# Attention scores: full passes of 128 rows, and the 32 or 64 rows left over in row groups of the TensorE array

## The chip, the cores and the metric

The kernel runs on one core of one Trainium2 chip. The metric is the device time of one execution in microseconds, as the median of several runs. The profile used below is of one further execution of the same program on the chip.

## The reference, cut to what matters

Two layers of a diffusion backbone are computed in 32-bit floats, over 1024 latent tokens (16 rows of 64) and 256 context tokens. Layer 0 has 8 heads of dense attention (the GQA heads, 64 features, two key heads) and 8 heads of neighbourhood attention (64 features, 8 rows by 16 columns of keys around each query, plus the context). Layer 1 has 16 heads of latent attention (MLA), whose queries and keys have 64 features without and 32 features with rotary embedding. Each attention is followed by a projection, a normalisation and a gated feed-forward layer with a convolution.

```python
HEAD_DIM = 64; A_HEADS = 8; A_KV_HEADS = 2; B_HEADS = 8
MLA_HEADS = 16; MLA_NOPE_DIM = 64; MLA_ROPE_DIM = 32

def one_block(qblk):                                    # dense attention, layers 0 and 1
    s = jnp.concatenate([jnp.einsum('bgrqd,bgkd->bgrqk', qblk, k),
                         jnp.einsum('bgrqd,bgcd->bgrqc', qblk, kc)], axis=-1)
    p = jax.nn.softmax(s.astype(jnp.float32) * scale, axis=-1).astype(v.dtype)
    return (jnp.einsum('bgrqk,bgkd->bgrqd', p[..., :length], v)
            + jnp.einsum('bgrqc,bgcd->bgrqd', p[..., length:], vc))

# neighbourhood attention, one row of queries, layer 0
s_nb = jnp.einsum('bhqd,bhrqkd->bhqrk', q_row, k_win).astype(jnp.float32) * scale + bias[None]
s_ctx = jnp.einsum('bhqd,bhcd->bhqc', q_row, kc).astype(jnp.float32) * scale

# layer 1
q = jnp.concatenate([q_nope, _rope(q_rope, cos, sin)], axis=-1)        # 64 + 32 features
k, v = up_kv(c_kv, _rope(k_r, cos, sin))                               # the 32 are shared by the heads
```

## The kernel before

TensorE works on float32r numbers here, and each 32-bit value that enters a product is split into a high and a low part, so that a product becomes a sum of products of parts. The scores of a head are made that way. For a GQA or neighbourhood head, the query tile `q` holds the 64 features of the high part over the 64 of the low part (128 rows), and the key tile `k` holds, twice, the high part in its first slot and the low part in its second. Two passes of 128 rows are summed: query tile by high keys, and query tile by low keys. For an MLA head the tiles have 96 rows and a slot for each part, and three passes of 96 rows are summed: high by high, high by low, low by high.

`attention()` works in units, a unit being a pair of query tiles of 128 queries. There are 4 units in a head: 32 units of GQA, 32 of the neighbourhood and 64 of MLA, and in layer 0 a context unit after the first pair of every second head. `seg` makes the scores of one query tile against a run of keys: it cuts the run at PSUM banks of 512 columns, and each piece becomes a function `go` that issues all the passes of that piece, one after the other, into its bank. For GQA and MLA the pieces of a unit have 512, 512, 256 (first tile), 256 and 512, 512 (second tile) columns; for the neighbourhood they have 384 and 256, and 256 and 384. The lists `la` and `lb` of these functions are spread over the places `sa` and `sb` of a schedule (`GQA_SCHED`, `NAT_SCHED`, `MLA_SCHED`, in units of a period). All steps of all units go into one heap by those places: scores on TensorE, maximum on VectorE, exponential on ScalarE, scaling on GpSimd, transposes on TensorE (`transpose`, L304), the split of the transposed exponentials (L311 to L320), the weighted sums on TensorE (`weighted`, L335) and the sum into `y` (`finish`). TensorE, ScalarE and VectorE then run in exactly that order.

The heads' tiles are loaded ahead: `prep` and `prep1` of head n + 1 are called with the second unit of head n, on the queue of SyncE (SP). In `prep1` the loads of MLA head 0 go to GpSimd's queue instead and into a pool of their own (`att1f`); those of the other heads use two buffers in turn (`att1k`). Layer 0's first head takes tiles that were loaded during the projections (`first`). The last unit's projections of layer 1 end in `up_q` and `up_kv`, which run through the helper `mm_acc` (L417); its rotary step for the shared key, `prt_k`, is a small product of 32 rows by 32 columns, and L730 spreads a row of four numbers over 128 partitions, with four-row weights.

The two lines by which a score is made:

```python
for pi, (q, k) in enumerate(u["passes"]):
    ...
    nc.tensor.matmul(
        u["s"][bank][:, c:e], q[:, qc], ks, start=pi == 0, stop=pi == len(u["passes"]) - 1
    )
```

Of the kernel before, what the change touches and what calls it, by code (L numbers as in the profile page):

```python
# [18 lines left out]
P = 128  # L19
D = 1024  # L20
# [13 lines left out]
# first of the 32 columns that 16 columns of queries look at  # L34
# [3 lines left out]
# places of the steps of a pair of query tiles, in units of the period  # L38
# [19 lines left out]
def attention(tc, pa, pp, ident, mone, units, engines=("tensor", "scalar", "vector")):  # L58
    """Softmax attention over pairs of query tiles.

    `units` make dicts: qt (query tiles), passes ((queries, keys) products whose sum is the score),
    v ([keys, tile, v_hi | v_lo]), y. A unit with "window" (w, bias) has the neighbourhood's queries of
    the w-th 16 columns, upper half over lower half, each against twelve rows of 32 columns. A unit
    with "context" has the context's queries of two heads and goes between two pairs.
    TensorE makes the scores of a pair, VectorE their maximum, ScalarE the exponentials and their
    sums; TensorE transposes the exponentials, ScalarE and VectorE (or GpSimd) split them into two
    float32r parts on the way out, and TensorE makes the weighted sums, which the reciprocal of
    the sum scales. Units come with a schedule that places these steps in time, in units of
    its period; the engines in `engines` keep that order.
    """  # L70
# [7 lines left out]
    def region(tag, sched):  # L78
        """PSUM for scores (sa, sb), transposed exponentials (t) and weighted sums (av)"""
# [9 lines left out]
    def plan_context(i, u, sched):  # L89
        """both heads' context queries, between two pairs"""  # L90
# [69 lines left out]
        # between the sums of two pairs  # L160
# [5 lines left out]
    def plan(i, u, sc):  # L166
# [11 lines left out]
        def seg(when, bank, c, k0, w, j, rows=None):  # L178
# [3 lines left out]
            lst = []  # L182
            while w:
                e = min(c + w, (c // 512 + 1) * 512)
                def go(c=c, e=e, k0=k0):
                    if bank not in u["s"]:
                        u["s"][bank] = region(bank, sc)
                    for pi, (q, k) in enumerate(u["passes"]):
                        if rows is None:
                            ks = k[:, k0 : k0 + e - c]  # L190
                        else:
                            w0 = WINDOWS[win]
                            ks = k[:, 0:NX].rearrange("p (r c) -> p r c", c=64)[:, rows : rows + 12, w0 : w0 + 32]
                        nc.tensor.matmul(  # L194
                            u["s"][bank][:, c:e], q[:, qc], ks, start=pi == 0, stop=pi == len(u["passes"]) - 1
                        )

                lst.append(go)
                w -= e - c
                k0 += e - c  # L200
                c = e
            when.extend(lst)

        la, lb = [], []
        if win is None:
            seg(la, "sa", 0, 0, 1024, 0)
            seg(la, "sa", 1024, NX, 256, 0)
            seg(la, "sa", 1280, NX, 256, 1)
            seg(lb, "sb", 0, 0, 1024, 1)
            segs = [[("sa", 0, 1280)], [("sb", 0, 1024), ("sa", 1280, 256)]]  # L210
        else:
            seg(la, "sa", 128, 0, 384, 0, rows=0)
            seg(la, "sa", 512, NX, 256, 0)
            seg(lb, "sb", 256, NX, 256, 1)
            seg(lb, "sb", 512, 0, 384, 1, rows=4)
# [58 lines left out]
        # blocks of 128 keys, shared by the query tiles that look at them, in groups of one bank  # L274
# [1639 lines left out]
```

## Time and profile before

| what | us |
|---|---|
| median of 3 runs | 3627.86 |
| lowest and highest run | 3622.21, 3631.36 |
| span of the profiled execution | 3624.5 |
| GQA scores, from the first to the last, on TensorE | 367.8 to 621 |
| neighbourhood scores | 634.3 to 797 |
| MLA scores | 2227.4 to 2739 |

The profiled execution lies 3.4 us below the median of the runs. The page gives busy times of the engines over the whole span; TensorE (PE) is far ahead. A matmul's listed duration runs from its start until its result has drained, so durations of successive matmuls overlap: what a matmul costs in a stream is the distance from its start to the next one's start, and it is read from the timeline. PEld is TensorE's weight load, which precedes every matmul.

### The profile page before, as it was taken

How to read it: one execution, taken by the hardware profiler on the slowest of the kernel's cores; microseconds unless marked ns; L12 is line 12 of the kernel's file. 1: busy time of each engine (PE TensorE's matmuls, PEld its weight loads, DVE VectorE, ACT ScalarE, POOL GpSimd, SP SyncE). 2: the span in 40 equal slices, each digit the busy share in tenths (PEclk: the TensorE clock that was granted, in tenths of full speed). 3: DMA queues.
4: the chain of work that ended last, by engine and by line, in shares of the span. 5: the costliest groups of instructions: out<-in, count | busy, mean ns of one | idle time of the engine just before them, and what ended most of it. 6: DMA issues, size and time to landing. Idle time of an engine off the chain costs nothing.

```text
span 3624.5 us, 50952 instructions
## 1 busy us (share of the span) xinstructions
PE 3444.8 (95%) x19450; PEld 2949.6 (81%) x19450; DVE 2252.0 (62%) x3434; ACT 1281.6 (35%) x2393; POOL 1668.7 (46%) x1804
## 2 busy tenths in 40 slices
PE   7998899979899999999998999999999999999997
PEld 5987787877788888888886787999997788888885
DVE  6687787873666666655455544777774555445555
ACT  4222777762411111111025334777773301111002
POOL 4532787643422222232223523888886533333333
PEclk9999999999999999999999999999999999999998
DMA  6367411664333322211104267233323211111111
GB/s 211 111 203 217 108 46 48 166 181 139 117 108 96 93 88 82 82 53 41 36 19 125 82 242 231 57 79 76 80 66 114 85 47 47 53 47 47 53 35 47
DMA packets 311952, 349.52 MB, mean 96 GB/s; under 512 B 19157, under 2 KB 233597, under 8 KB 311709
## 3 DMA queue, kind: packets, MB, share of 16 engines
q1 hardware_dynamic: 298508, 319.66, 30.4%
q10 hardware_dynamic: 11424, 18.94, 1.4%
q0 software_dynamic: 1776, 7.67, 0.6%
q8 instruction: 153, 2.51, 0.3%
q14 instruction: 91, 0.74, 0.1%
HBM read 275.04 MB, written 71.11 MB: 96 GB/s over the span
## 4 chain that ended last, share of the span: by engine, by line
PE 74%; POOL 8%; DVE 8%; issue 5%; DMA 4%; ACT 2%; SPq 0%; ACTq 0%; POOLq 0%; DVEq 0%
PE pu L417 29%; PE pd L417 15%; PE psum L194 7%; PE psum L335 5%; PE pso L417 4%; PE psum L304 4%; POOL p L264 3%; PE psq L417 2%; PE ps_f L417 2%; PE ps_tu L417 1%; DVE aa L552 1%; PE pw L417 1%; POOL pl L312 1%; DMA bias<-in_l_rpb_dram 1%; POOL st L261 1%
## 5 line engine op out<-in xcount | busy, mean ns | idle before, releaser
L1400 DVE SCALAR_TENSOR_TENSOR acc<-pd,mods,acc 128x512 f32<-128x512 f32 (+1 forms) x800 | 525.0, 697 | 267.0 <-PE pd L417 252.3
L408 POOL TENSOR_SCALAR fh_u<-fr_u 128x1024 fp32r<-128x1024 f32 x88 | 95.0, 1079 | 857.6 <-PE pu L417 479.9
L417 PE MATMUL pd<-ah,fh_d 128*128 128x512 f32 (+1 forms) x880 | 331.7, 377 | 6.3 <-DVE acc L1400 3.8
L417 PE MATMUL pd<-al,fh_d 128*128 128x512 f32 (+1 forms) x880 | 326.0, 370 | 0.5 <-DVE al L412 0.5
L417 PE MATMUL pd<-ah,fl_d 128*128 128x512 f32 (+1 forms) x880 | 325.9, 370 | 0.0
L194 PE MATMUL psum<-k,q 96*128 96x512 f32 (+1 forms) x1152 | 272.3, 373 | 6.7 <-DMA k<-kr_scr 4.0
L417 PE MATMUL pu<-h_1l,fh_u 128*128 128x512 f32 x704 | 275.1, 391 | 2.1 <-POOL h_1l L412 2.1
L417 PE MATMUL pu<-h_0h,fh_u 128*128 128x512 f32 x704 | 275.3, 391 | 0.0
L417 PE MATMUL pu<-h_0h,fl_u 128*128 128x512 f32 x704 | 275.0, 391 | 0.0
L417 PE MATMUL pu<-h_0l,fh_u 128*128 128x512 f32 x704 | 274.9, 391 | 0.0
L417 PE MATMUL pu<-h_1h,fh_u 128*128 128x512 f32 x704 | 274.3, 390 | 0.0
L417 PE MATMUL pu<-h_1h,fl_u 128*128 128x512 f32 x704 | 274.0, 389 | 0.0
L1381 DVE TENSOR_TENSOR cv<-cv,pu 128x1280 f32<-128x1280 f32 (+1 forms) x44 | 59.6, 1355 | 295.7 <-PE pu L417 289.1
L194 PEld LDWEIGHTS psum<-k,q 96*128 96x128 f32 x1152 | 196.4, 192 | 35.3 <-issue 4.4
L412 POOL TENSOR_TENSOR fl_u<-fr_u,fh_u 128x1024 fp32r<-128x1024 f32 x88 | 212.4, 2413 | 7.3
L552 DVE SCALAR_TENSOR_TENSOR aa<-aw,silu_late,aa 128x512 f32<-128x512 f32 x224 | 190.5, 880 | 37.1 <-DMA aw<-in_l_w_ada_dram 34.9
L417 PEld LDWEIGHTS pd<-ah,fh_d 128*128 128x128 f32 x880 | 166.1, 189 | 58.2 <-DVE acc L1400 5.1
L1377 ACT ACTIVATE cv<-cv 128x1280 f32<-128x1280 f32 (+1 forms) x44 | 51.4, 1169 | 443.0 <-DVE cv L1373 443.0
L264 POOL TENSOR_SCALAR p_m<-p_m,st_m 128x640 f32<-128x640 f32 x256 | 201.8, 801 | 12.6
L1367 ACT ACTIVATE cv<-pu,vec 128x1280 f32<-128x1280 f32 (+1 forms) x44 | 58.2, 1322 | 417.5 <-PE pu L417 417.5
L320 DVE TENSOR_TENSOR pl_m<-psum,ph_m 128x512 fp32r<-128x512 f32 x256 | 175.0, 684 | 37.7 <-ACT ph_m L314 36.7
L304 PE MATMUL psum<-ident,p_m 128*128 128x128 f32 x1280 | 192.9, 273 | 2.5 <-DVE pl_m L320 2.2
(499 smaller groups left out, 9817.1 us busy)
## 6 DMA issues: line engine op xcount, KB each, us to landing
aw<-in_l_w_ada_dram SPq DMA_DIRECT2D x96, 512.0 KB
fr_u<-in_l_w_up_dram SPq DMA_DIRECT2D x88, 512.0 KB
fr_d<-in_l_w_down_dram SPq DMA_DIRECT2D x44, 512.0 KB
fr_o<-in_l_w_out_dram SPq DMA_DIRECT2D x30, 512.0 KB
v<-v_scr SPq DMA_DIRECT2D x17, 640.0 KB
k_b<-k_scr SPq DMA_DIRECT2D x16, 640.0 KB
v_scr<-vev SPq DMA_DIRECT2D x40, 256.0 KB
k<-k_scr SPq DMA_DIRECT2D x15, 640.0 KB
```

Source lines behind the costliest of these rows:

```text
L194: nc.tensor.matmul(u["s"][bank][:, c:e], q[:, qc], ks, start=pi == 0, stop=pi == len(u["passes"]) - 1)
L264: nc.gpsimd.tensor_scalar(pt, pt, st[:, j, 7:8], 0.0, op0=ALU.mult, op1=ALU.add)
L304: nc.tensor.transpose(tp[:, off + bi * P : off + bi * P + P], pts[j][:, c : c + P], ident)
L320: nc.vector.tensor_tensor(pl[:, :w], tps[g][:, :w], ph[:, :w].bitcast(F32), ALU.subtract)
L335: nc.tensor.matmul(u["av"][:, q0 : q0 + bw], u["v"][:, kt, :], m[:, off : off + bw], start=first and part == 0, stop=last and part == 1, s ...
L408: nc.gpsimd.tensor_scalar(dst, src, 1.0, 0.0, op0=ALU.mult, op1=ALU.add)
L412: e.tensor_tensor(dst, src, hi.bitcast(F32), ALU.subtract)
L417: nc.tensor.matmul(ps, s, m, start=i == 0, stop=i == n - 1)
L552: nc.vector.scalar_tensor_tensor(accs[c], w, sck, accs[c], op0=ALU.mult, op1=ALU.add)
L1367: nc.scalar.activation(cv, g[:, :nt], AF.Identity, bias=vec(l, "cb", f), scale=vec(l, "w1", f))
L1381: nc.vector.tensor_tensor(cv, cv, v[:, :nt], ALU.mult)
L1400: nc.vector.scalar_tensor_tensor(acc[m][ci], ps[:, :cn], mod(l, ci // 2, 5, m), acc[m][ci], op0=ALU.mult, op1=ALU.add)
```

## The change

The passes of a score become full passes of 128 rows and a remainder, which is a matmul of 64 rows (GQA, neighbourhood) or 32 rows (MLA) of the array.

- GQA and neighbourhood: one full pass, (high over low) queries by high keys, and a remainder of 64 rows, high queries by low keys. The remainder is either on rows 0 to 63, from `q` and `k`, or on rows 64 to 127, from a new tile `ql` that holds the high queries there; pieces take the two in turn. The product of the two low parts is left out. A tile `ql` is loaded for each head, one more transfer of 64 rows. The context's queries keep their two passes.
- MLA: the 3 x 96 = 288 rows are packed into two full passes of 128 rows and a remainder of 32 rows, which is loaded four times, on rows 0, 32, 64 and 96. The tiles get 128 rows and three slots. A head's queries and keys are then loaded by 18 transfers instead of 4, and even and odd heads have one buffer each, in `att1f` and `att1k`.
- Order on TensorE: `seg` returns the full passes and the remainders apart, and `beside` places the remainders of neighbouring pieces behind their full passes as one step. The pieces of a step go to different banks and, as far as there are, to different row groups. Each unit of GQA and MLA has three such steps (of 3, 1 and 2 matmuls), each unit of the neighbourhood two (of 2 and 2).

```diff
-                def go(c=c, e=e, k0=k0):
+                n = n0 + len(lst)
...
+                def go(c=c, e=e, keys=keys):
                     if bank not in u["s"]:
                         u["s"][bank] = region(bank, sc)
                     for pi, (q, k) in enumerate(u["passes"]):
...
+                        nc.tensor.matmul(u["s"][bank][:, c:e], q[:, qc], keys(k), start=pi == 0, stop=False)
+
+                def last(c=c, e=e, keys=keys, n=n):
+
+                    q, k = u["thin"][n % len(u["thin"])]
+                    nc.tensor.matmul(u["s"][bank][:, c:e], q[:, qc], keys(k), start=False, stop=True)
...
+        def beside(*pieces):
+
+            full, thin = zip(*pieces)
+            full, thin = sum(full, []), sum(thin, [])
+
+            def rest():
+                for f in thin:
+                    f()
+
+            return [*full, rest]
+
         if win is None:
-            seg(la, "sa", 0, 0, 1024, 0)
-            seg(la, "sa", 1024, NX, 256, 0)
-            seg(la, "sa", 1280, NX, 256, 1)
-            seg(lb, "sb", 0, 0, 1024, 1)
+            la = beside(seg("sa", 0, 0, 1024, 0, 0), seg("sa", 1024, NX, 256, 0, 2))
+
+            la += beside(seg("sa", 1280, NX, 256, 1, 2))
+            lb = beside(seg("sb", 0, 0, 1024, 1, 0))
             segs = [[("sa", 0, 1280)], [("sb", 0, 1024), ("sa", 1280, 256)]]
         else:
...
+            la = beside(seg("sa", 128, 0, 384, 0, 0, rows=0), seg("sa", 512, NX, 256, 0, 1))
+            lb = beside(seg("sb", 256, NX, 256, 1, 0), seg("sb", 512, 0, 384, 1, 1, rows=4))
...
-            return q
...
+            return q, load_low(src, h, name)
+
+        def load_low(src, h, name):
+            ql = pa.tile([P, NT], F32R, name=f"ql_{name}", tag="ql", bufs=3)
+            nc.sync.dma_start(ql[64:P].bitcast(F32), src[0, 64 * h : 64 * h + 64, :])
+            return ql
...
-                    "passes": [(st["q"], st["k"][0]), (st["q"], st["k"][1])],
+                    "passes": [(st["q"][0], st["k"][0])],
+                    "thin": [(st["q"][0][0:64], st["k"][1][0:64]), (st["q"][1][64:P], st["k"][1][64:P])],
...
-            pool, load = (pk, nc.sync) if hd else (pf, nc.gpsimd)
+            pool, load = pk if hd % 2 else pf, nc.sync if hd else nc.gpsimd
...
-            q = pool.tile([96, 2, NX], F32R, name=f"q1_{hd}", tag="q", bufs=2 if hd else 1)
-            k = pool.tile([96, 2, NT], F32R, name=f"k1_{hd}", tag="k", bufs=2 if hd else 1)
+            q = pool.tile([P, 3, NX], F32R, name=f"q1_{hd}", tag="q", bufs=1)
+            k = pool.tile([P, 3, NT], F32R, name=f"k1_{hd}", tag="k", bufs=1)
...
-                (q[0:64], q1_scr[g][:, 64 * j : 64 * j + 64]), (q[64:96], qr_scr[g][:, 32 * j : 32 * j + 32]),
-                (k[0:64], k1_scr[g][:, 64 * j : 64 * j + 64]), (k[64:96], kr_scr),
+                *((q[0:64, i], qn[:, 0]) for i in range(2)), *((q[64:96, i], qr[:, 0]) for i in range(2)),
+                (q[96:P, 0], qr[:, 1]), (q[96:P, 1], qn[0:32, 1]),
+                (k[0:64, 0:2], kn), (k[64:96, 0:2], kr), (k[96:P, 0], kr[:, 0]), (k[96:P, 1], kn[0:32, 0]),
+                *((q[r : r + 32, 2], qn[32:64, 1]) for r in range(0, P, 32)),
+                *((k[r : r + 32, 2], kn[32:64, 0]) for r in range(0, P, 32)),
...
-                    "passes": [(qh, kh), (qh, kl), (ql, kh)],
+                    "passes": [(q[:, i, :], k[:, i, :]) for i in range(2)],
+                    "thin": [(q[r : r + 32, 2, :], k[r : r + 32, 2, :]) for r in range(0, P, 32)],
```

TensorE, the scores of one MLA unit's list `la`, in the middle of layer 1. In these rows L194 is a score before, `ident,p_m` is a transpose, and `ph_m,v` begins a weighted sum. Before:

```order
L194 MATMUL psum<-k_12_25257,q_12_25256 128x512 x6
L194 MATMUL psum<-k_12_25257,q_12_25256 128x256 x3
L304 MATMUL psum<-ident,p_m_0_0_25663 128x128
L304 MATMUL psum<-ident,p_m_0_1_25640 128x128
L304 MATMUL psum<-ident,p_m_0_0_25663 128x128
L304 MATMUL psum<-ident,p_m_0_1_25640 128x128
L194 MATMUL psum<-k_12_25257,q_12_25256 128x256 x3
L335 MATMUL psum<-ph_m_0_1_25761,v_12_25255 128x256
```

And the same place of another head now, where L198 is a full pass and L203 a remainder:

```order
L198 MATMUL psum<-k_11_25023,q_11_25022 128x512 x4
L198 MATMUL psum<-k_11_25023,q_11_25022 128x256 x2
L203 MATMUL psum<-k_11_25023,q_11_25022 128x512 x2
L203 MATMUL psum<-k_11_25023,q_11_25022 128x256
L198 MATMUL psum<-k_11_25023,q_11_25022 128x256 x2
L320 MATMUL psum<-ident,p_m_0_0_25443 128x128
L320 MATMUL psum<-ident,p_m_0_1_25420 128x128
L320 MATMUL psum<-ident,p_m_0_0_25443 128x128
L320 MATMUL psum<-ident,p_m_0_1_25420 128x128
L203 MATMUL psum<-k_11_25023,q_11_25022 128x256
L351 MATMUL psum<-ph_m_0_1_25555,v_11_25021 128x256
```

Where each piece had three passes in a row, the remainders of the first three pieces now stand together between full passes, and the fourth piece's remainder stands alone between the transposes and the weighted sum.

GpSimd's queue, the loads of MLA head 0 at the start of layer 1's attention, with the semaphores that each waits for (a name with DMASW is the landing of an earlier transfer of this queue, one of eight in turn). Before:

```order
L1783 DMA q_0_20647<-q_scr_103 64x2x1024 [waits DMAHW7_49,PE_49]
L1783 DMA q_0_20647<-qr_scr_107 32x2x1024 [waits DMAHW4_49]
L1783 DMA k_0_20648<-k_scr_111 64x2x1280 [waits Pool_49]
L1783 DMA k_0_20648<-kr_scr 32x2x1280
L1784 DMA v_0_20646<-v_scr_115 128x10x128 [waits DMAHW7_49,DMAHW6_49,DMAHW4_49]
```

Now, the first ten rows of the same place (four more of the queries' remainder, four of the keys' and the values follow):

```order
L1817 DMA q_0_20679<-q_scr_103 64x1024 [waits DMAHW7_49,PE_49]
L1817 DMA q_0_20679<-q_scr_103 64x1024
L1817 DMA q_0_20679<-qr_scr_107 32x1024 x2
L1817 DMA q_0_20679<-qr_scr_107 32x1024 [waits DMAHW4_49]
L1817 DMA q_0_20679<-q_scr_103 32x1024
L1817 DMA k_0_20680<-k_scr_111 64x2x1280 [waits PE_49,Pool_49]
L1817 DMA k_0_20680<-kr_scr 32x2x1280
L1817 DMA k_0_20680<-kr_scr 32x1280 [waits DMASW0_49]
L1817 DMA k_0_20680<-k_scr_111 32x1280 [waits DMASW1_49]
```

From the ninth transfer on, each waits for the landing of the one eight before it.

## Rows read from the trace of the kernel before

**Rows 1.** The page: busy time by engine, and the chain that ended last.
```profile
PE 3444.8 (95%) x19450; PEld 2949.6 (81%) x19450; DVE 2252.0 (62%) x3434; ACT 1281.6 (35%) x2393; POOL 1668.7 (46%) x1804
...
PE 74%; POOL 8%; DVE 8%; issue 5%; DMA 4%; ACT 2%; SPq 0%; ACTq 0%; POOLq 0%; DVEq 0%
```
**Rows 2.** Busy time by stretch: GQA, neighbourhood, steady MLA; then clock, DMA share, GB/s.
```profile
367.00:627.00 260.00, 236.73 (x1676) 208.92 (x1676) 204.60 (x301) 199.62 (x419) 206.96 (x304) 0.99 0.25 62
632.00:803.00 171.00, 147.47 (x1089) 137.26 (x1090) 131.85 (x283) 127.13 (x307) 105.17 (x161) 0.97 0.64 172
2262.00:2705.00 443.00, 443.00 (x3197) 415.68 (x3196) 342.33 (x497) 350.45 (x717) 388.86 (x552) 1.00 0.32 73
```
**Rows 3.** TensorE's waits between 632 and 803 us: total us, times, longest.
```profile
PE psum L335 <- DVE y L368: 10.6, 14, 3.4
```
**Rows 4.** Timeline of TensorE in MLA: start us, duration us, operation, count; 8.04 us apart.
```profile
2452.81 1.63 PE L194 MATMUL psum<-k,q 96*128 96x512 f32 x6
...
2455.12 1.97 PE L194 MATMUL psum<-k,q 96*128 96x512 f32 x9
2456.92 0.60 PE L304 MATMUL psum<-ident,p_m 128*128 128x128 f32 x4
2457.28 0.60 PE L194 MATMUL psum<-k,q 96*128 96x256 f32 x3
2457.72 0.28 PE L335 MATMUL psum<-ph_m,v 128*128 128x256 f32 x1
2457.84 0.28 PE L335 MATMUL psum<-pl_m,v 128*128 128x256 f32 x1
...
2460.85 1.63 PE L194 MATMUL psum<-k,q 96*128 96x512 f32 x6
```
**Rows 5.** Timeline of TensorE in layer 1's first projection, around a 32-row matmul.
```profile
1953.71 0.39 PE L417 MATMUL pw<-h_0h,fh_wi 128*128 128x512 f32 x1
1953.93 0.39 PE L417 MATMUL pw<-h_0l,fh_wi 128*128 128x512 f32 x1
1954.25 0.41 PE L417 MATMUL prt_k<-reh_k,perm 32*32 32x512 f32 x1
1954.59 0.50 PE L417 MATMUL pw<-h_0h,fl_wi 128*128 128x512 f32 x1
1954.93 0.40 PE L417 MATMUL pw<-h_0h,fh_wi 128*128 128x512 f32 x1
```
**Rows 6.** The weight loads of the same place.
```profile
1954.25 0.10 PEld L417 LDWEIGHTS prt_k<-reh_k,perm 32*32 32x32 f32 x1 [0.35 <-issue]
1954.59 0.19 PEld L417 LDWEIGHTS pw<-h_0h,fl_wi 128*128 128x128 f32 x1 [0.24 <-issue]
1954.70 0.19 PEld L417 LDWEIGHTS pw<-h_0h,fh_wi 128*128 128x128 f32 x1
```
**Rows 7.** Timeline of TensorE around eight matmuls of four rows and two columns.
```profile
53.22 0.40 PE L788 MATMUL ps_f<-hh,wl_in 128*128 128x512 f32 x1
53.55 1.05 PE L730 MATMUL ps_mr<-pick,row 4*128 4x2 f32 x8
54.53 0.39 PE L788 MATMUL ps_f<-hh,wh_in 128*128 128x256 f32 x1
```
**Rows 8.** Line L1783, the loads of MLA heads: issue ns, and waits behind them.
```profile
L1783 SPq DMA_DIRECT2D q<-q_scr x15: 586/586/2985, 2230.6 to 2675.0; - x15
...
L1783 POOL DMA_DIRECT2D k<-kr_scr x1: 554/554/554, 2216.5 to 2216.5; - x1
...
  PE psum L194: 4.0, 1
...
DMA to landing us min/median/max: 6.0/8.1/10.8
```
**Rows 9.** One stretch in which MLA head 3 is loaded: clock, DMA share, GB/s.
```profile
2292.00:2294.00 2.00, 1.00 1.11 227
```

More of the change, by code (lines that the diff above doesn't have):

```diff
@@ L176, in plan, with seg, keys @@
         pts = [None] * nq
-        def seg(when, bank, c, k0, w, j, rows=None):
+        def seg(bank, c, k0, w, j, n0, rows=None):
             qc = slice(u["qt"][j] * P, u["qt"][j] * P + P)
-            lst = []
+            lst, thin = [], []
             while w:
                 e = min(c + w, (c // 512 + 1) * 512)
-                def go(c=c, e=e, k0=k0):
+                n = n0 + len(lst)
+                def keys(k, c=c, e=e, k0=k0):
+                    if rows is None:
+                        return k[:, k0 : k0 + e - c]
+                    w0 = WINDOWS[win]
+                    return k[:, 0:NX].rearrange("p (r c) -> p r c", c=64)[:, rows : rows + 12, w0 : w0 + 32]
+                def go(c=c, e=e, keys=keys):
                     if bank not in u["s"]:
@@ L188, in go @@
                     for pi, (q, k) in enumerate(u["passes"]):
[L189 to L196, printed above, removed]
+                        nc.tensor.matmul(u["s"][bank][:, c:e], q[:, qc], keys(k), start=pi == 0, stop=False)
+                def last(c=c, e=e, keys=keys, n=n):
+                    q, k = u["thin"][n % len(u["thin"])]
+                    nc.tensor.matmul(u["s"][bank][:, c:e], q[:, qc], keys(k), start=False, stop=True)
                 lst.append(go)
+                thin.append(last)
                 w -= e - c
@@ L201, in seg @@
                 c = e
[L202 to L204 removed]
+            return lst, thin
+        def beside(*pieces):
[5 more added lines that the diff above has]
+            return [*full, rest]
         if win is None:
[L206 to L209 removed]
+            la = beside(seg("sa", 0, 0, 1024, 0, 0), seg("sa", 1024, NX, 256, 0, 2))
+            la += beside(seg("sa", 1280, NX, 256, 1, 2))
+            lb = beside(seg("sb", 0, 0, 1024, 1, 0))
             segs = [[("sa", 0, 1280)], [("sb", 0, 1024), ("sa", 1280, 256)]]
         else:
[L212 to L215, printed above, removed]
+            la = beside(seg("sa", 128, 0, 384, 0, 0, rows=0), seg("sa", 512, NX, 256, 0, 1))
+            lb = beside(seg("sb", 256, NX, 256, 1, 0), seg("sb", 512, 0, 384, 1, 1, rows=4))
             segs = [[("sa", 128, 640)], [("sb", 256, 640)]]
@@ L1090, in prep @@
                 g = hd // 4
-                st["q"] = load_q(q_scr[hd // 2], hd % 2, f"a{hd}") if hd else first[2]
+                st["q"] = (
+                    load_q(q_scr[hd // 2], hd % 2, f"a{hd}") if hd else (first[2], load_low(q_scr[0], 0, "a0"))
+                )
                 if hd % 4 == 0:
@@ L1132, in make @@
                     st = state[h]
-                    heads.append({"passes": [(st["q"], st["k"][0]), (st["q"], st["k"][1])], "v": st["v"], "vc": 8 if h < 8 else 16})
+                    heads.append({"passes": [(st["q"][0], st["k"][0]), (st["q"][0], st["k"][1])], "v": st["v"], "vc": 8 if h < 8 else 16})
                 return {"name": f"c{hd}", "context": heads, "y": state["y", hd // 2]}
```

8 lines of the change are left out of this document (6 added, 2 removed).

## The prediction

> **What bounds the kernel now.** I read the page first. TensorE is busy for 95% of the span and carries 74% of the chain that ended last [rows 1], so time added to or taken from its stream shows in the end, unless TensorE waits where it falls. I therefore looked at the three stretches that the change touches, by windows [rows 2]. In MLA's steady part TensorE is busy for all of 443 us at a granted clock of 1.00, that is 2.4 GHz: every tenth of a microsecond there counts in full. In the GQA stretch it is not busy for 260.00 - 236.73 = 23 us, in the neighbourhood stretch for 171.00 - 147.47 = 24 us, the largest single wait in the latter being 10.6 us for VectorE's `y` [rows 3].
>
> Then the price of one matmul, from distances between starts. In a stream, 512 columns take 0.225 us (0.22 in [rows 5]) and 256 columns 0.12 [rows 4]. This closes: six of the one and three of the other would be 1.71 us, and from 2455.12 to 2456.92 they take 1.80 [rows 4]; three of 256 would be 0.36 and take 0.44. The extra 0.08 to 0.09 is paid by the first matmul behind a group of transposes. Weight loads are hidden in these streams. An MLA unit takes 2460.85 - 2452.81 = 8.04 us.
>
> **What the change removes.** Only the last pass of each piece. Full passes cost by their columns, so 96 or 128 rows make no difference to their price. The removed passes of an MLA unit are 512, 512, 256 columns (0.57 us), 256 (0.12) and 512, 512 (0.45), 1.14 us in all; GQA's are the same; the neighbourhood's are two times 384 and 256. For 384 I have no undisturbed row and take 0.17, between the other two, so 0.29 each.
>
> **What it adds: the switch.** A remainder is a 32- or 64-row matmul between 128-row ones. The trace has this pattern in a few places, and one is shown: `prt_k`, 32 rows and 512 columns, in a stream of full matmuls of 512 columns [rows 5]. The starts are 1953.93, 1954.25, 1954.59 and 1954.93: three matmuls in 1.00 us where three full ones take 0.675. The 0.32 us more stand in three parts: 0.10 before the small one starts, 0.11 behind it, and 0.11 for the next one's weights. The weight loads say why [rows 6]: the small matmul's load does not start with the matmul before it, as in a stream, but 0.32 us after that, together with its own matmul, and the same holds for the full one behind it. PEld's releaser is "issue", so no data was late. A second example, eight four-row matmuls with 128-column weights, starts 0.33 us behind a 512-column one [rows 7], again 0.10 late. The remainders' weights have 128 columns, `prt_k`'s 32. A load of 128 columns takes 0.11 (1954.59 to 1954.70, [rows 6]), one of 32 a quarter, so 0.08 more is exposed. I price a step of remainders at **0.40 us** besides its columns.
>
> **What it gives: matmuls side by side.** No row shows two row groups at work at once, so this is bounded. At best the matmuls of a step run wholly together and the longest counts; at worst they run one after the other and nothing is saved. I take the middle case, by the row nearest to it: each needs its own 128-column weights, and matmuls of only two columns still follow each other by (54.53 - 53.55) / 8 = 0.12 us [rows 7], close to the load's 0.11. So a second row group starts 0.11 later and a third 0.22.
>
> - MLA, three steps in a unit. 512, 512, 256: 0.11 + 0.225 = 0.34 in place of 0.57, saved 0.23. 512, 512: 0.335 in place of 0.45, saved 0.12. The lone 256 saves nothing. Added 3 x 0.40 = 1.20, less 0.08 at the lone one, which stands behind transposes and had paid that before [rows 4]. Net 1.20 - 0.08 - 0.35 = +0.77 us, times 64 units: **+49 us**.
> - GQA, three steps. There are two row groups, so the third piece returns to the first one's and must wait for its end and its weights: 0.225 + 0.11 + 0.12 = 0.455, saved 0.115; the pair saves 0.115. Net 1.20 - 0.23 = +0.97, times 32: **+31 us**.
> - Neighbourhood, two steps: 0.80, saved 0.06 (384 then 256) and 0.01 (256 then 384). Net +0.73, times 32: **+23 us**.
>
> The Trainium skill's page "TensorE: Matmul & The Clock Gate" (Measured speedup vs the span model) gives 3.07 times for four row groups of 32 rows and 512 columns. That would be a start about 0.02 us after the other (an estimate from that figure) instead of 0.11, and the sum below would be about 18 us smaller. No row here shows it.
>
> **What is moved or loaded.** In MLA a head's queries and keys grow from 96 rows and two slots to 128 rows and three: 3.5 MB instead of 1.8, in 18 transfers instead of 4, with 0.66 MB of values as before. At the 227 GB/s that a head's load reaches now [rows 9] 4.2 MB take 18.5 us, and 18 issues of 0.59 us [rows 8] 10.6 us. A head lasts 4 x 8.04 = 32 us now and longer then, and the buffers change hands as before, so this is hidden; its cover is the head's own scores. What is queued behind a waiting transfer on SP is only the next head's tiles.
>
> The start of layer 1's attention has no cover. Head 0's loads are on GpSimd's queue, 0.55 us each, and land after 6.0 to 10.8 us; TensorE already waits 4.0 us for the last of them [rows 8]. With 18, the ninth may only start when the first has landed, and so on in eights; the first remainder needs the copies on its two row groups, which are among the last. Two rounds of landing in place of one are 8 us (the median), and some of it again for the third. From 3 us (only more bytes) to 15 (two further rounds): I take **+10**. Behind these transfers GpSimd's own queue holds only head 0's first scalings, which need the scores anyway. In layer 0 the first head's `ql` is one transfer more ahead of the first remainder: +1.
>
> Other engines get slack, since TensorE is their source. Where TensorE waited for them, part of its added time disappears in the wait: half of the neighbourhood stretch's 24 us, **-12** (between 0 and all 24).
>
> **Sum.** 49 + 31 + 23 + 10 + 1 - 12 = +102 us on the span of 3624.5, which is 3.4 below the median of the runs: 3627.9 + 102 = **3730 us**. With everything side by side the steps give 35 + 24 + 18 = 77, less 24 of waits, plus 3: +56, 3684. With nothing saved: 72 + 38 + 26 = 136, plus 15: +151, 3779.
>
> **Rivals.**
>
> - The row groups run one after the other and each exposes its weights. Then 3, 3 and 2 loads of 0.11 a unit come on top of "nothing saved", 39 us: about 3800. For it: in [rows 6] a load waits until the array is free. Against: that is at a change between shapes, not between row groups. Chance 0.13.
> - Faster. The switch costs nothing, because the small weights are loaded beside running full matmuls, and the row groups run together. Each MLA unit then loses 0.57 us, each GQA unit 0.45, each neighbourhood unit 0.24: 36 + 14 + 8 = 58 us less, plus 11 at the starts: 3580 us. It decides at a price of the step of about 0.15 us. For it: `prt_k` changes columns too (32), the remainders do not. Against: the four-row matmuls have all 128 columns and start as late [rows 7]. Chance 0.08. The skill's page "TensorEngine Tiling (Array Packing)" (Theoretical Speedup) promises up to 2 or 4 times for 64 or 32 rows; its Key Properties add that a change of tiling mode drains the engine. The 0.10 us before and behind `prt_k` agree with the latter.
> - The switch costs half, 0.20 us, as the schedule puts it where weights are late anyway. MLA +0.17, GQA +0.37, neighbourhood +0.33 a unit: 33 us, with starts and waits 32: 3660 us. Chance 0.08.
> - The MLA loads become the bound, if 32-row transfers, eight at a time, reach only half the rate: 39 us a head, 4 more than the 35 that I expect a head to take, 60 us in all: 3790. Against: a DMA share of 0.32 now [rows 2]. Chance 0.03.
>
> **How the numbers follow.** My forecast, a time between 3684 and 3779, has 0.68. The range runs from 3665, which takes in part of the half-price case, to 3795, which takes in the loads and the lower part of the serial case. Changes below 0.3% (11 us) can hardly be told from none here. Slower by more than that: 0.68 + 0.13 + 0.03 + most of the 0.08, together 0.89. Within: 0.03. Faster: 0.08.
>
> **What the profile of the changed kernel would show.** An MLA unit of about 8.8 us, still with TensorE busy throughout; by 8.6 everything ran side by side, by 9.2 nothing did, and below 8.04 the switch is free. Around each step of remainders, weight loads that start only after the full matmul before, about 0.32 us behind its start, and the same for the full one behind. Inside a step, starts 0.11 us apart. A first MLA score some 5 us later than now and a first remainder some 5 us after that. Neighbourhood waits for `y` mostly gone. The prediction is wrong if a remainder's weights are loaded during the full matmul ahead of it.

## The result, and the profile after

| | before | after |
|---|---|---|
| median of four runs, us | 3625.03 | 3709.47 |
| lowest and highest, us | 3615.21, 3631.36 | 3707.10, 3710.53 |
| span of the profiled execution, us | 3624.5 | 3705.2 |

The changed kernel is slower, by a ratio of 1.0237 with a 95% interval of 1.022 to 1.0255, or 84 us by the medians and 81 by the two profiled executions. The forecast was 3730, the range 3665 to 3795.

The first two parts of the page, which answer [rows 1]. TensorE is as far ahead as before and carries the same share of the chain; it does more.

```profile
PE 3517.4 (95%) x19450; PEld 2905.7 (78%) x19450; DVE 2256.9 (61%) x3434; ACT 1283.9 (35%) x2393; POOL 1676.8 (45%) x1818
...
PE 75%; POOL 8%; DVE 7%; issue 4%; DMA 3%; ACT 2%; ACTq 0%; SPq 0%; POOLq 0%; DVEq 0%
```

The three stretches by windows, as in [rows 2]: GQA, neighbourhood, and MLA in its steady part.

```profile
365.00:640.00 275.00, 253.75 (x1658) 198.55 (x1659) 204.81 (x298) 198.22 (x414) 207.09 (x304) 0.98 0.28 73
649.00:841.00 192.00, 163.88 (x1106) 131.56 (x1104) 135.63 (x285) 129.02 (x311) 103.43 (x159) 0.98 0.59 155
2300.00:2790.00 490.00, 490.00 (x3292) 403.05 (x3291) 351.79 (x511) 360.49 (x738) 399.98 (x566) 1.00 0.55 121
```

MLA is TensorE without a gap, at the same clock. The busy share alone does not prove that (run 10 below is as busy in a slower unit), but the starts do: beyond the 0.61 us that a unit gains they leave no room for waits. TensorE's free time in the two stretches of layer 0, 21 and 28 us, is together no smaller than before (23 and 24). From where each stage begins in the two traces, the 81 us lie as follows: GQA +17.7, neighbourhood +25.7, start of layer 1's attention +3.1, its units +43.1, and -8.8 at the start of the program and between the layers. Of the neighbourhood's 25.7, 18.1 lie between its first score and its last weighted sum, and 7.6 between that sum and the first matmul of layer 0's projection. An MLA unit takes 8.647 us instead of 8.04, a GQA unit 7.80 instead of 7.27, a neighbourhood unit 4.78 instead of 4.05 to 4.17.

The steps of remainders, on the timeline of TensorE (start us, duration us, operation, count): an MLA unit with its three steps and the beginning of the next unit, 8.65 us later, and the weight loads (PEld) of the last place, as in [rows 6].

```profile
2495.41 1.17 PE L198 MATMUL psum<-k,q 128*128 128x512 f32 x4
...
2499.21 0.50 PE L203 MATMUL psum<-k,q 32*128 32x512 f32 x3
2499.64 0.51 PE L198 MATMUL psum<-k,q 128*128 128x256 f32 x2
2499.98 0.60 PE L320 MATMUL psum<-ident,p_m 128*128 128x128 f32 x4
2500.51 0.38 PE L203 MATMUL psum<-k,q 32*128 32x256 f32 x1
2500.82 0.39 PE L351 MATMUL psum<-ph_m,v 128*128 128x256 f32 x1
...
2504.06 1.17 PE L198 MATMUL psum<-k,q 128*128 128x512 f32 x4
2505.16 0.50 PE L203 MATMUL psum<-k,q 32*128 32x512 f32 x2
2505.59 0.39 PE L351 MATMUL psum<-ph_m,v 128*128 128x256 f32 x1
2505.81 0.28 PE L351 MATMUL psum<-pl_m,v 128*128 128x256 f32 x1
```

```profile
2504.61 0.19 PEld L198 LDWEIGHTS psum<-k,q 128*128 128x128 f32 x1
2505.16 0.18 PEld L203 LDWEIGHTS psum<-k,q 32*128 32x128 f32 x2 [0.36 <-issue]
2505.59 0.19 PEld L351 LDWEIGHTS psum<-ph_m,v 128*128 128x128 f32 x1 [0.25 <-issue]
```

L203 is a remainder. Two remainders of 512 columns take 0.50 us together, as long as one: they and their weights start within 0.004 us of each other. The last step starts 0.318 us behind the start of the last full matmul (0.225 in a stream), the next matmul 0.43 behind the step, and its successor 0.22 behind that instead of 0.12. That is 0.09 ahead, 0.20 behind and 0.10 for the next weights: **0.39 us for a step**, where the forecast had 0.40. The whole unit gives the same. It is 0.61 us longer, without the 1.14 of its third passes and with 0.225 + 0.225 + 0.12 = 0.57 of remainder columns, so 1.18 us stand for three steps. The expectations below went by 0.42, a figure that counts 0.08 too much at the lone step behind the transposes (see the price of a step, further down).

GQA, whose third piece has to return to the first one's row group:

```profile
583.81 0.49 PE L203 MATMUL psum<-k_a,q_a 64*128 64x512 f32 x1
583.82 0.50 PE L203 MATMUL psum<-k_a,ql_a 64*128 64x512 f32 x1
584.15 0.28 PE L203 MATMUL psum<-k_a,q_a 64*128 64x256 f32 x1
584.36 0.39 PE L198 MATMUL psum<-k_a,q_a 128*128 128x256 f32 x1
```

Neighbourhood: VectorE's rows of a unit, and then TensorE's waits in the stretch (us in all, times, longest us), as in [rows 3].

```profile
701.83 0.82 DVE L250 CUSTOM_DVE_ANT_0 p<-psum,bias 128x640 f32<-128x640 f32 x1 [0.48 <-PE psum L203]
...
704.11 0.82 DVE L250 CUSTOM_DVE_ANT_0 p<-psum,bias 128x640 f32<-128x640 f32 x1 [0.33 <-PE psum L203]
704.86 0.08 DVE L250 DVE_READ_ACCUMULATOR2_ANT st<- 128x1 f32 x1
704.99 0.42 DVE L384 TENSOR_TENSOR y<-psum,avt 64x256 f32<-64x256 f32 x1
```

```profile
PE psum L351 <- DVE y L384: 13.9, 24, 2.4
PE psum L148 <- DVE y L384: 6.0, 4, 1.5
```

The maximum (L250) waits for the remainders, the sum into `y` stands behind it on VectorE, and TensorE's next weighted sums wait for `y`: 24 waits where there were 14.

Behind the neighbourhood, layer 0's projection starts later: TensorE's wait ahead of its first matmul (us in all, times, longest us), and the issue of its first weights on SyncE's queue. Before:

```profile
PE pso L417 <- ACT y_0h L404: 2.4, 1, 2.4
782.45 0.40 SPq L1231 DMA_DIRECT2D fr_first<-in_l_w_out_dram  x1
```

Now:

```profile
PE pso L433 <- ACT y_0h L420: 10.0, 1, 10.0
SPq L1255 <- DVE pl L336: 24.4, 1, 24.4
839.75 0.39 SPq L1255 DMA_DIRECT2D fr_first<-in_l_w_out_dram  x1
```

The transfer was issued 25 us ahead of the stage's last weighted sum (807.3) and is now issued with it (840.4), because it waits for the stage's last splits on VectorE; the parts of `y` are loaded behind it. From the last weighted sum to the 200th matmul of the projection it is 51.4 us instead of 47.7, so 3.7 us stay lost.

### The profile page after: what moved, and what is told of

Its sections match the earlier page's. It is cut to its first block, busy times and chain, and to the rows that moved or that the text cites. A ratio compares the mean times of both kernels' runs of the same rounds, so it can differ in the third digit from the quotient of the medians.

```text
span 3705.2 us, 51271 instructions
## 1 busy us (share of the span) xinstructions
PE 3517.4 (95%) x19450; PEld 2905.7 (78%) x19450; DVE 2256.9 (61%) x3434; ACT 1283.9 (35%) x2393; POOL 1676.8 (45%) x1818
## 4 chain that ended last, share of the span: by engine, by line
PE 75%; POOL 8%; DVE 7%; issue 4%; DMA 3%; ACT 2%; ACTq 0%; SPq 0%; POOLq 0%; DVEq 0%
PE pu L433 28%; PE pd L433 14%; PE psum L351 6%; PE psum L198 5%; PE psum L320 5%; PE pso L433 4%; POOL p L280 3%; PE psum L203 2%; PE ps_tu L433 2%; PE psq L433 2%; PE ps_f L433 2%; PE pw L433 1%; DVE aa L568 1%; POOL pl L328 1%; POOL st L277 1%
## 5 line engine op out<-in xcount | busy, mean ns | idle before, releaser
L198 PE MATMUL psum<-k,q 128*128 128x512 f32 (+1 forms) x768 | 201.9, 385 | 9.3 <-DMA k<-kr_scr 7.1
L1401 ACT ACTIVATE cv<-cv 128x1280 f32<-128x1280 f32 (+1 forms) x44 | 51.4, 1169 | 442.6 <-DVE cv L1397 442.6
L267 ACT ACTIVATE p_m<-psum,st_m 128x1024 f32<-128x1024 f32 (+2 forms) x192 | 187.0, 984 | 15.4 <-DVE st_m L260 14.5
```

Of the source, the lines that this page charges most:

```text
L198: nc.tensor.matmul(u["s"][bank][:, c:e], q[:, qc], keys(k), start=pi == 0, stop=False)
L267: nc.scalar.activation(pt, src if bias is None else pt, AF.Exp, bias=st[:, j, 2:3], scale=1.0 if bias is None else -1.0, accum_out=st[:, j ...
```

## The experiments

Times are compared with the kernel before on the same chip (3621 to 3626 us). "Span" is the profiled execution's; that of before is 3624.5, of after 3705.2. Runs 1 to 6 are one execution each, 7 to 12 four to nine.

**1. The same order and loads, but full matmuls as remainders.** It separates the order from the row groups. All 128 rows are used, so the remainder's product is counted more than once.

```diff
-  "thin": [(q[r : r + 32, 2, :], k[r : r + 32, 2, :]) for r in range(0, P, 32)],
+  "thin": [(q[:, 2, :], k[:, 2, :])],          # and layer 0 likewise
```

> The changed kernel with the same order, loads and tiles, but every remainder as a matmul over all 128 rows: in layer 0 the old second pass, in MLA the four copies of the 32 rows at once, so that the MLA remainder is counted four times in the sum. No row groups and no change of shape are left. If the price is in the change of shape: an MLA unit goes from 8.65 us back to 8.04, a GQA pair from 7.80 to 7.27, a neighbourhood pair from 4.78 to about 4.1, and only the later start of MLA is left, some 8 us: about 3633. Rival, the order or the larger loads cost the time: the neighbourhood pairs stay above 4.4 and the total above 3650.

3644.8 us (span 3643.0). MLA 8.06 and GQA 7.28 us a unit, as before; neighbourhood 4.35 to 4.47. So the row-group shape itself is what costs in MLA and GQA, but 0.3 us of the neighbourhood's 0.7 come without any row group: the rival's point is half met. From the first neighbourhood score to the last weighted sum it takes 182.3 us (172.9 before, 191.0 after), and the projection starts 9.9 us behind that, as late as in the changed kernel. The first MLA score comes 3.1 us later relative to the work ahead of it, and the MLA stage is 6.6 longer though its units are not: both lie at its start.

**2. All remainders in the first row group.**

```diff
-  "thin": [(q[r : r + 32, 2, :], k[r : r + 32, 2, :]) for r in range(0, P, 32)],
+  "thin": [(q[0:32, 2, :], k[0:32, 2, :])],          # and layer 0 likewise
```

> The changed kernel with every remainder on the first row group (rows 0 to 31, or 0 to 63), so that nothing runs side by side. If the row groups run together, as starts 3 ns apart in the trace say: a second matmul in the same group starts 0.34 us behind the first, as GQA's third one does. MLA +0.89 us a unit (57 us), GQA +0.67 (21), neighbourhood +0.45 (14): about 3800. Rival, the recorded starts are only the issue and the matmuls run one after the other already: no change, 3709.

3767.95 us (span 3766.2). MLA 9.22, GQA 8.23 to 8.27, neighbourhood 5.01 us a unit: 0.57, 0.44 and 0.23 more than after. Row groups do run side by side; the rival (no difference) falls. But the loss was two thirds of what I expected, and the trace says why: a step of three, and the weight loads of it.

```profile
2546.43 0.62 PE L198 MATMUL psum<-k,q 128*128 128x512 f32 x3
2546.99 0.84 PE L203 MATMUL psum<-k,q 32*128 32x512 f32 x3
2547.76 0.51 PE L198 MATMUL psum<-k,q 128*128 128x256 f32 x2
```

```profile
2546.98 0.53 PEld L203 LDWEIGHTS psum<-k,q 32*128 32x128 f32 x3
```

Inside a step of one group the next weights are loaded while a matmul of that group runs: the second load starts 0.11 us behind the first matmul's start, the third together with the second matmul. The starts are 0.337 and then 0.236 us apart, so the second matmul still pays 0.11 and the third next to nothing.

**3. Each MLA remainder in a step of its own**, six instead of three.

```diff
+            if len(u["thin"]) == 4:
+                return [f for pair in zip(full, thin) for f in pair]
```

> The changed kernel with MLA's remainders each directly behind the full passes of its own piece: six steps a unit in place of three, the same matmuls. If a step costs about 0.42 us whatever is in it: 3 x 0.42 = 1.26 more, and the 0.57 of side by side are lost: +1.83 us a unit, an MLA unit of 10.5, 117 us: about 3826. Rival, the price lies in the matmuls and not in the step: only the 0.57 are lost, 36 us, 3746.

3814.85 us (span 3813.1), an MLA unit 10.36 us: +1.72 for three more steps. The columns that no longer overlap are 0.57 of it, so 0.38 us stand for each added step, close to the 0.39 above. The price is paid by the step.

**4. Two steps in an MLA unit**: the lone piece of 256 columns joins the step ahead of it, in the row group and bank of the other 256.

```diff
-            la = beside(seg("sa", 0, 0, 1024, 0, 0), seg("sa", 1024, NX, 256, 0, 2))
-            la += beside(seg("sa", 1280, NX, 256, 1, 2))
+            la = beside(*pieces)          # the three segs; the last one does not clear the bank
```

> The changed kernel with MLA's lone remainder of 256 columns moved into the step before it, on the row group of the other 256 of its bank, behind which it runs: two steps a unit in place of three. If the price is by the step: 0.42 less and 0.12 more for the matmul that is second in its group, an MLA unit of about 8.35 us, 14 to 19 us less in all: 3690 to 3695. Rival, the price is by the matmul: no change, 3709.

3676.97 us (span 3675.2), an MLA unit 8.16 us, 0.49 less, more than the theory's 0.3: the second 256 of its row group ran beside the 512s and cost nothing, so price and columns of the lone step (0.39 + 0.12) both went.

```profile
2601.50 0.51 PE L203 MATMUL psum<-k,q 32*128 32x512 f32 x4
2601.94 0.38 PE L350 MATMUL psum<-ph_m,v 128*128 128x256 f32 x1
```

**5. Layer 0 as before.**

```diff
-  "passes": [(st["q"][0], st["k"][0])],
-  "thin": [(st["q"][0][0:64], st["k"][1][0:64]), (st["q"][1][64:P], st["k"][1][64:P])],
+  "passes": [(st["q"][0], st["k"][0]), (st["q"][0], st["k"][1])],
```

> Only layer 1's part of the change; layer 0 is the kernel before. Theory (the parts add up): GQA pair of tiles 7.27 us and neighbourhood 4.05 to 4.17 as before, MLA unit 8.65, start of layer 1's attention 8 us later: 38 + 8 above the kernel before, about 3671 us. Rival (the loss at layer 0 also shifts what layer 1 costs, or the reverse): outside 3660 to 3680.

Layer 0's `ql` is not loaded either. 3674.3 us (span 3672.2), units 7.27, 4.04 to 4.18 and 8.647; the projection starts 2.6 us behind the last weighted sum, as before. The parts add up: 48 of the 81 us are layer 1, 33 layer 0.

**6. The neighbourhood's scores earlier in the fixed order.**

```diff
-    "period": 4.1, "sb": (-2.129, -2.002), "sa": (-1.77, -1.658),
+    "period": 4.1, "sb": (-2.249, -2.122), "sa": (-1.89, -1.778),
```

> The changed kernel with the neighbourhood's score steps 0.12 of a period earlier in the fixed order. Theory (a good part of the neighbourhood's loss is VectorE, whose maximum now waits for a remainder step that ends late, so that its sum into y is late and TensorE waits for it): with the scores earlier the waits for y go, a unit takes about 4.45 us instead of 4.78 to 4.83, and the whole about 3700. Rival (the loss is the price of the steps alone): unit unchanged, 3709.

Units fell to 4.49 us, as expected, but the whole came to 3707.7 (span 3705.6), the rival's time. The two rows below are waits in the neighbourhood stretch, of TensorE and of VectorE.

```profile
PE psum L351 <- DVE y L384: 9.4, 5, 4.3
...
DVE p L250 <- DMA bias<-in_l_rpb_dram: 8.8, 2, 5.6
```

The many short waits for `y` are gone, 5 stand for 24, so the ring of remainders, maximum, `y` and weighted sums was the cause of that part of the unit's loss. Two of the rest are long: at the change of a head's bias table VectorE waits 8.8 us for the transfer (4.8 in the changed kernel). From the first neighbourhood score to the first projection behind the stage it takes 196.9 us instead of 201.2; those 4.3 us the execution lost ahead of the stage, whose first GQA score came 5.0 us later, in code that is the same. Spans of different executions differ by that much at the start (362 to 370 us in the runs of this study). The projection still starts 10.0 us behind the last weighted sum.

**7 and 8. One step of all six remainders in an MLA unit**, on row groups 0, 1, 2, 3, 2, 0, with layer 0 as before; the second of the two kernels also keeps head 0's 96-row passes and four loads.

```diff
-            la = beside(seg("sa", 0, 0, 1024, 0, 0), seg("sa", 1024, NX, 256, 0, 2))
-            la += beside(seg("sa", 1280, NX, 256, 1, 2))
-            lb = beside(seg("sb", 0, 0, 1024, 1, 0))
+            lb = seg("sb", 0, 0, 1024, 1, 3)
+            la = beside(*pieces, lb)          # its one step stands at the end of la; lb keeps the full passes
```

> Layer 0 as before the change; in layer 1 all six remainders of an MLA unit stand in ONE step (at the end of the first list of scores), on row groups 0, 1, 2, 3, 2, 0, in place of three steps; the first maximum of the unit's second half is scheduled 0.25 of a period later. Theory (the price is by the step, 0.42 us, and groups overlap): a unit pays 0.42 + 2 x 0.225 of columns = 0.87 us in place of the 1.14 of the third passes, so 7.75 us instead of 8.04, 18 us less in 64 units; the start of layer 1's attention still costs 8. About 3615 us, 0.3% under the kernel before. Rival (the later scores stall VectorE's maxima, and these TensorE): the unit stays above 8.04 and the time above 3633.

> As the kernel with one step of remainders in an MLA unit, but head 0 of layer 1 keeps its three passes of 96 rows and its four loads, so nothing is added at the start of layer 1's attention. Theory (price by the step; the start's cost is the 18 loads of head 0): a first MLA score at the time of the kernel before, a unit of 7.75 us, about 3609 us, 0.45% under the kernel before and 6 to 8 under the other. Rival (the maxima stall): above 3630.

3660.28 us (ratio 1.010, 1.0085 to 1.0116) and 3661.87 (1.0107, 1.009 to 1.0125): both slower than before, with a unit of 8.562 us. The rival's numbers hold. TensorE's and VectorE's largest waits in the first one, 300 us of MLA:

```profile
PE psum L329 <- DVE pl_m L345: 15.3, 35, 0.4
...
DVE pl_m L345 <- ACT ph_m L339: 61.4, 35, 1.8
DVE st_m L266 <- PE psum L206: 11.8, 35, 0.4
```

The step itself cost what was expected: with 0.09 ahead, 0.66 in it and 0.10 behind it 0.85 us stand for 1.14. But the unit's maxima wait for one late step (0.3 us a unit), VectorE's split of the transposed exponentials (`pl_m`) waits 1.8 us a unit for ScalarE's part of it (`ph_m`), and TensorE waits for `pl_m` in all 35 units. That the late step is at the root of these waits is argued from their order; the later place of the one maximum was not tried without the step.

Keeping head 0's loads gave back less than expected: the first score still waits 6.1 us for `kr_scr` (7.0 with 18 loads, 4.0 before [rows 8]). GpSimd's queue says why; the second kernel's load of the keys, and that of the kernel before:

```profile
2222.64 0.58 POOL L1826 DMA_DIRECT2D k<-k_scr  x1 [3.81 <-PE psq L442]
```

```profile
2215.92 0.60 POOL L1783 DMA_DIRECT2D k<-k_scr  x1
```

The keys' loads wait 3.81 us for a matmul of the query projection (`psq`), which they did not before; with 18 loads they wait for it too, 1.98 us behind the first six. The key tile has 128 rows and three slots in this kernel as well, so its place is likely to be one that TensorE still reads; a smaller tile was not tried.

**9 and 10. A first new order for layer 1, with one step, and the same order without remainders.**

```diff
+    "sb": (-1.735, -1.73), "sa": (-1.92, -1.774), "sc": (-1.701, -1.694), "th": -1.647,
+    "m0": -1.483, "mx": -1.213, "mc": -1.285, "e0": -1.382, "ec": -0.969, "ex": -1.070, ...
```

`sc` places the two pieces of 256 columns, `th` the step.

> The kernel before mla_order in this study that keeps head 0 of layer 1 as it was (one step of six remainders in an MLA unit), with another fixed order in layer 1: the 1280-wide maximum and exponential of the first query tile come before those of the second, the two 256-column pieces are made after the 512-column ones, and the step of remainders stands ahead of the transposes. Theory: the one-step kernels lost their gain in a ring, remainders, maxima (1.6 us), exponentials (1.1, 0.46, 1.3 with a copy of 0.6 between), the next unit's scores (1.5) and remainders again; with the long exponential first the ring has 1.5 us less and TensorE is the bound. It then pays 0.09 ahead of the step, 0.66 in it and 0.10 behind it in place of 1.14 of third passes: 7.75 to 7.9 us a unit instead of 8.04, 60 units, and 2 us at the start: 7 to 15 us under the kernel before, about 3613. Rival (the step itself costs more than it saves wherever it stands): a unit above 8.04, a time above 3628.

> The kernel before with the new fixed order of layer 1 alone, three passes of 96 rows everywhere. Theory: TensorE is busy all the time there already, so an order can't give anything: MLA unit 8.04, time 3622 to 3632. Rival (the order is what helps, not the remainders): a unit of 7.9 or less.

3665.9 us (1.0122, 1.0107 to 1.0137) and 3661.03 (1.011, 1.0093 to 1.0127), units 8.595 and 8.594. Both theories fall: an order alone can lengthen an MLA unit nearly as much as the change did (8.647), and here it set the time with and without remainders. With the order alone TensorE counts as busy for 300.00 of 300 us, although its starts leave 0.55 us a unit unused: a matmul's listed duration hides such short waits. One row, VectorE's wait in 300 us of MLA, names the place:

```profile
DVE st_m L271 <- ACT p_m L281: 31.1, 35, 0.9
```

The maximum over 256 columns waits 0.89 us in every unit until the 1280-wide exponential has ended, although it needs nothing from it. They read the same PSUM bank, and that this is the reason is argued: no run gave the 256 columns a bank of their own. The Trainium skill's page "PSUM — Partial Sum Buffer" (PSUM bank collisions raise a hardware error) says that the compiler's scheduler adds a dependency between instructions of different engines that touch the same bank and partitions, reads too; a wait of 0.89 us agrees with that.

**11 and 12. A second order, with that bank rule kept in mind, with and without the step.** The 1024-column maximum, which reads other banks, goes ahead of the 256-column one. Layer 0 and MLA head 0 are as before the change.

```diff
+    "sb": (-1.9351, -1.7892), "sa": (-2.1334, -1.9884), "sc": (-1.8239, -1.8189), "th": -1.7872,
+    "m0": -1.7119, "mx": -1.4589, "mc": -1.3013, "e0": -1.4391, "ec": -1.0315, "ex": -1.2285, "t": -0.3948,
+    "l": -0.2617, "td": 0.7631, "av": 0.2849, "avd": 0.7952, "fin": 1.0552, ...
```

> One step of six remainders in an MLA unit, head 0 of layer 1 as it was, with a second fixed order in layer 1. The first one put the 256-column maximum of the second tile ahead of the 1024-column one; it shares a PSUM bank with the 1280-wide exponential, and the runs mla_order and order_only both show it waiting 0.89 us a unit for that exponential to end. Now the 1024-column maximum, in other banks, comes first and runs beside the exponential, and a unit's transposes and sums are spread again. Theory: TensorE has no wait left and pays 0.09 ahead of the step, 0.66 in it and 0.10 behind it in place of 1.14 of third passes: 7.7 to 7.85 us a unit instead of 8.04, in 60 units 11 to 20 us less, 1 to 2 back at the start: about 3607. Rival (the step costs more than it saves wherever it stands): a unit above 8.04 and a time above 3626.

> The kernel before with this second order in layer 1 alone, three passes of 96 rows everywhere. Theory: TensorE is busy all the time in the kernel before, so an order alone gives nothing: MLA unit 8.04 to 8.1, time 3620 to 3628. Rival (the order is what helps): a unit of 7.9 or less.

With the step: **3607.70 us, ratio 0.9958 (0.9944 to 0.9971)**, 15 us under the kernel before and 102 under the changed one. The order alone: 3630.54, ratio 1.0022 (1.0012 to 1.0031), unit 8.17. So the gain is the remainders', and it needs the order. An MLA unit takes 7.71 us; windows and timeline of it:

```profile
2400.00:2700.00 300.00, 300.00 (x2259) 263.37 (x2259) 243.23 (x351) 251.11 (x507) 272.59 (x389) 1.00 0.61 134
```

```profile
2505.41 1.65 PE L198 MATMUL psum<-k,q 128*128 128x512 f32 x8
2506.99 0.73 PE L206 MATMUL psum<-k,q 32*128 32x512 f32 x6
2507.64 0.66 PE L334 MATMUL psum<-ident,p_m 128*128 128x128 f32 x4
```

TensorE is busy throughout, and six remainders with their step take 2507.64 - 2506.99 = 0.65 us, with 0.09 ahead of it and 0.06 behind, where transposes follow. In the kernel before the same six pieces take 1.14; the 0.34 between is the unit's gain (8.04 to 7.71).

## Why the prediction was right, and where it was wrong

**What bounds the kernel**: right. TensorE was and is the chain; in MLA each unit's added 0.61 us shows 63 times.

**The price of a step of remainders, 0.40 us**: right, 0.39. `prt_k` [rows 5, 6] and the four-row matmuls [rows 7] gave the pattern: a late start, a late successor, exposed weights. The rival by which the switch is free, or half the price, falls with runs 3 and 4. In GQA two of three steps are cheaper, 0.35 and 0.36, because transposes, whose weights take 0.14 instead of 0.19, follow them. What the forecast took off again, 0.08 at the lone step behind transposes, was a misreading: in [rows 4] four transposes and three passes of 256 columns take 0.80 us, which is their price in a stream (4 x 0.109 + 3 x 0.12). The first matmul there takes 0.08 longer only because it starts 0.08 earlier. The lone remainder costs 0.39 like the others. The Trainium skill's page "TensorEngine Tiling (Array Packing)" (Key Properties) says that a change of tiling mode drains the engine; the trace agrees, and puts a number to it.

**Side by side, the second 0.11 us later and the third 0.22**: the step that failed, in size. In different row groups the weights are loaded together and the starts are 0.003 us apart. The term was taken from two-column matmuls in one row group [rows 7], and run 2 shows that this is what a second matmul of the same group pays. It accounts for MLA: columns of 0.57 instead of 0.79 us a unit, 0.22 less, against which stands the 0.08 above, so +0.61 instead of +0.77, 38 us instead of 49. In GQA the third piece came 0.34 behind the first, as forecast, and took 0.21 to the next start; columns and prices give +0.64 instead of +0.97. The unit grew by 0.53, 17.7 us in all instead of 31; most of the other 0.1 is a group of four transposes that took 0.47 us and takes 0.38 now. The Trainium skill's page "TensorE: Matmul & The Clock Gate" (Measured speedup vs the span model), which the prediction set beside this, was the better source for this term: four remainders in four groups start 0.003 us apart in runs 7 and 11. That it would have made the sum 3712 where 3709 was measured is luck, since other terms were off both ways. The serial rival (3800; its own terms add up to 3818) falls with run 2.

**Neighbourhood: +23 for the steps and -12 of waits that vanish**: wrong in mechanism, 18.1 up to the last weighted sum instead of 11, and 7.6 more ahead of the projection. The deferred remainders end later than the old second passes, and what was a wait of TensorE for `y` became a ring that TensorE itself delays. Run 1 shows 0.3 us a unit without any row group (9.4 of the 18.1), and with the scores earlier run 6 takes 0.3 a unit out again. The forecast said that other engines get slack; it did not ask what they wait for.

**Start of layer 1's attention, +10**: 3.1 to the first score and 4.9 more in the first units, 8 together, near the forecast but not by its two rounds of landing alone. The first remainder came 3.6 us behind the first score, not 5. Run 8 kept head 0's four transfers, and 2 of the 3 us stayed: the keys' loads are held back by a matmul. In the first units the late copies of the remainders cost 1.9 us of waits; the rest is mostly the clock, of which the forecast had nothing:

```profile
2227.40:2247.40 20.00, 17.00 (x64) 13.51 (x65) 9.18 (x12) 7.98 (x16) 8.83 (x14) 0.74 1.07 287
```

```profile
2265.70:2285.70 20.00, 15.99 (x39) 9.55 (x40) 4.91 (x6) 3.08 (x6) 6.43 (x10) 0.50 1.05 274
```

These are the 20 us behind the first score, before and after. TensorE had waited 4.0 us before and 7.1 after, and its granted clock is then 0.74 in the mean before and 0.50, that is 1.2 GHz, after. For 16 busy us the difference is 3.8 us at full speed, an estimate from these two rows.

**MLA loads hidden**: right. TensorE's starts show no wait in the steady units, with a DMA share of 0.55.

**The layer-0 `ql`, +1**: nothing to be seen at the start; the first score came 2.6 us earlier, inside what executions differ by. But all runs with `ql` start the projection 9.5 to 10.3 us behind the last weighted sum, and those without it (5, 7, 11, 12) 2.6 us, as before. Its three buffers take 15 KB of each partition during layer 0's attention, which would push the projection's first tiles into places that are in use until the end. That is argued: the runs with `ql` also have the new order in layer 0.

Together the terms were 102 us and came to 81: 24 too many in MLA and GQA, 15 too few in the neighbourhood and ahead of the projection, 3 too many at the two starts, and some 9 us less outside the stages. Of these 9, about 4 are waits for the parts of `y` that moved from behind the projection's first matmul to ahead of it; 5 are no more than executions differ by. So the sum came as near as it did partly because errors of opposite sign met. The sign was right for the stated reason. That a form of the same change could be faster stood in the prediction only as a free switch; it came another way, by one step in place of three and an order that lets the other engines follow.

## What to carry to other kernels

Row groups save columns, but every return to full matmuls costs a fixed price, here 0.39 us in a stream: count the steps, not the matmuls, and gather as many remainders as there are row groups and banks in one step. Work that is put off ends later for its consumers, so before deferring it look at which engine waits for its end, what stands behind that engine's wait, and whether TensorE waits for that. A tile that grows may delay a later stage, if it takes the place in which that stage would have loaded ahead (argued here, not shown): look at when the next stage's first transfers are issued. An order tuned for one set of steps is not the order for another, and it has to be tried without the change as well, or the order's effect is taken for the change's.

## What the runs showed that was not expected

- Matmuls in different row groups start 0.002 to 0.004 us apart, weights included; in one row group 0.337 and then 0.236 us (512 columns), the second load starting 0.11 us into the first matmul and the third with the second matmul.
- A 256-column matmul in a row group that already had one ended within the time of the 512-column ones beside it (0.51 us for all four).
- Short waits of TensorE do not show as idle time in a stream: its busy share was 1.00 in units of 8.04 and of 8.59 us.
- TensorE's granted clock was 0.50 for 20 us behind a wait of 7.1 us, and 0.74 in the mean behind one of 4.0 us.
- A maximum on VectorE waited 0.89 us a unit for an exponential on ScalarE that reads another part of the same PSUM bank.
